# A hybrid encoder step: the beginning loaded in pairs of tiles, the odd mixer's normalisation split into shorter pieces, and the last output tile finished in two halves

## The chip, the cores and the metric

The kernel runs on one core of a Trainium2 chip. The metric is the device time of one execution in microseconds (us). The core has a matrix engine (PE, with its weight loads listed as PEld), a vector engine (DVE), a scalar engine (ACT), a general engine (POOL), and SP, which here issues DMAs; ACT issues some too.

## The reference, cut to what matters

Two layers over 384 tokens (256 of a prompt and 8 x 16 of samples), 1024 features, everything in fp32:

```python
x = x + 0.5 * swiglu(rmsnorm(x, g1), wg, wu, wd)      # ffn1, 1024 -> 2816 -> 1024
x = x + mixer(rmsnorm(x, g))                          # layer 0: even mixer, layer 1: odd mixer
x = x + 0.5 * swiglu(rmsnorm(x, g2), wg, wu, wd)      # ffn2
# odd mixer
u, vv, ga, gb = split(h @ w_in)
vv = layernorm(gelu(vv), ln_g, ln_b);  yc = gelu(u) * spatial_gate(vv, ws, bs)
cd = causal_dwconv(ga * sigmoid(gb), width 31)
yd = silu(layernorm(cd + dw_b, cn_g, cn_b))
y  = concat(yc, yd) @ w_out
# at the very end
y = rmsnorm(x, final_g)
```

## The kernel before, in words

Activations lie with features on the 128 partitions and the 384 tokens along the free dimension, so `x` is eight tiles `xT[k]` of 128x384. Every product is made three times: each fp32 operand is split into a rounded part and a rest (`xh`, `xl` for activations, `hi`, `lo` for weights), and `mm3` adds high x high, low x high and high x low in one PSUM bank. The split of a tile is a copy on ACT (the high part) and a subtraction on DVE (the rest).

**The stream.** All weights come as pieces of 128x1024, in order, through `Stream`: SP issues the load of a piece into one of four `raw` buffers, `fill_split` makes its `hi` (ACT, L247) and `lo` (DVE or POOL, L249) in one of three buffers each, and `get` hands out a piece, issues loads further ahead, and splits two pieces ahead of the one handed out. A new `hi` thus waits until PE is done with the piece three places earlier.

**The order of the work** is written out by hand. `proj_a` makes two 128x384 results (two pieces), `proj_b` four, `proj_tok` three of 128 tokens x 512 columns. Inside them `tick` and `tock` advance a clock, `clock['n']`; side work is hung on it with `at(n, fn)`, whole numbers in the middle of a piece, halves at its end. Each engine works through its instructions in program order. Results of PE go into four banks of the kind `pbank` and four of the kind `bank`; a `pbank` can be written again only when the evacuation of its last content is done.

**The beginning** (L314 to L542). ACT's queue loads `pcol` (all per-feature columns, 98 KB); SP's queue loads `x` and the first two weight pieces in turns, the first two feature tiles one by one, the others in pairs. Eight matmuls of ones run meanwhile (L517). A loop over the eight feature tiles `k` makes `xh` (ACT, L520), the piece's part `hi` (ACT, L267), `lo` (POOL, L268), `xl` (DVE, L522), and PE's six matmuls of `k` (L525, L532, L533), the last four one step behind.

**The RMS factor** is a chain: `rstd_split`, `rstd_sums` (a sum over partitions on PE, then a diagonal picked out and reduced on DVE, a power of -1/2 on POOL, four small DVE steps that refine it, a diagonal product, a split), `rstd_spread` (PE, ACT). `first` (L557) evacuates the first two pairs of results of the first ffn, where that factor was not yet there.

**The odd mixer** has PE ticks 0 to 3 for `vv` (`proj_tok`), 4 to 11 for `ga, gb` (`glu`), 12 to 15 for `u`, 16 to 19 for the first half of the output projection (`ych`, `ycl`: four pieces, called A to D below, A and B for the first four results, C and D for the other four), 20 to 23 for the second (`ydh`, `ydl`: E to H). Convolutions 1 to 3 run on PE at ticks 9, 11, 13 (`conv`), convolution 0 as `taps` on DVE. The layer norm of `cd` hangs on the clock:

```python
        at(LN[0], ln_1)                            # 14: mean, centred cd, squares
        at(LN[1], ln_2)                            # 15: sum of the squares, split
        at(LN[2], lambda: rstd_sums(onesc))        # 16.5
        at(LN[3], ln_3)                            # 18: factor, 4 x (product, silu, split)
```

The gates `gate(i)` (two at tick 16) give `ych[i]`, `ycl[i]`: a product on DVE, then ACT's copy, then DVE's rest.

**The end** (`last`). For each 512-column half `hf` and 128 tokens `t` PE sums 22 products; the last three pieces of the second half are held back so that the three `t` end one after the other. `evac` adds to `x` and squares, `norm` makes the factor and the two output halves, which SP stores.

Of the kernel before, what the change touches and what calls it, by code (L numbers as in the profile page):

```python
# [42 lines left out]
P = 128  # L43
NT = 384
# [8 lines left out]
LN = (14, 15, 16.5, 18)  # L53
# [6 lines left out]
TP = (2, 2, 2, 2, 8, 2, 2, 2, 7, 2)  # L60
# [54 lines left out]
def _layout(x):  # L115
# [9 lines left out]
    def feat(a, n):  # L125
# [9 lines left out]
        'x': feat(tok, KD),  # L135
        'cols': cols,
# [16 lines left out]
_INS = [('w', (len(_pieces()), P, 1024)), ('x', (P, KD, NT)), ('cols', (P, NCOL)), ('ck', (8, P, 4, NP)),  # L153
# [68 lines left out]
class Stream:  # L222
# [56 lines left out]
def encoder_step(ctx, tc, d_w, d_x, d_cols, d_ck, d_cv, d_clf, d_ssc, d_scc, d_wfl, d_ebf, d_lng, d_lnb, d_wst,  # L279
# [51 lines left out]
    A.activation(warm, warm, AF.Copy)  # L331
# [51 lines left out]
    def rsqrt(out, v, n, pw=P):  # L383

        G.tensor_tensor(out, v, nhalf[:pw, 0:n], op=ALU.pow)  # L385
        t = tmp(8)[:pw]
# [22 lines left out]
    def rstd_sums(scale=None):  # L409
# [11 lines left out]
        rsqrt(rc[:, 0:3], v[:, 0:3], 3)  # L421
        dg = tmp()
        V.tensor_tensor(dg.rearrange("p (t q) -> p t q", q=P), id3,
                        rc[:, 0:3].unsqueeze(2).to_broadcast([P, 3, P]), op=ALU.mult)
        rbox['d'] = split_tmp(dg)
        rbox['rc'] = rc
# [89 lines left out]
    for _ in range(8):  # L516
        mm(ps_first[0][:, 0:P], lhsT=ones1, rhs=ones1, start=True, stop=True)  # L517
    for k in range(KD + 1):
        if k < KD:
            A.activation(xh[k], xT[k], AF.Copy, scale=col('ffn1_g', k))  # L520
            st.part_split(k // 4, k % 4)
            V.scalar_tensor_tensor(xl[k], xT[k], col('ffn1_g', k), xh[k].bitcast(F32),  # L522
                                   op0=ALU.mult, op1=ALU.subtract)
            for n in range(2):
                mm(ps_first[n][:, 0:NT], lhsT=st.hl[k // 4][0][:, k % 4, n * P:(n + 1) * P], rhs=xh[k],  # L525
                   start=k == 0, stop=False)
        if k > 0:
            q = k - 1
            hi, lo = st.hl[q // 4]
            for n in range(2):  # L530
                c = slice(n * P, (n + 1) * P)
                mm(ps_first[n][:, 0:NT], lhsT=hi[:, q % 4, c], rhs=xl[q], start=False, stop=False)  # L532
                mm(ps_first[n][:, 0:NT], lhsT=lo[:, q % 4, c], rhs=xh[q], start=False, stop=q == 7)  # L533
        if k in (3, 7):
            tick()
# [4 lines left out]
    adma(out=cb, in_=c_big)  # L540
    for k in range(KD):
        square(k, V)  # L542
# [5 lines left out]
    def ffn(rp, gnext, lnext, extra=None, ps0=None, fresh=True):  # L548
# [469 lines left out]
    def odd(pre, first_piece, gnext, lnext):  # L1018
# [83 lines left out]

        def ln_sum():
# [31 lines left out]
        def conv_sum(i):  # L1135
# [270 lines left out]
```

## Time and profile before

| | |
|---|---|
| median of 3 runs | 1444.8 us (1443.97 to 1445.63) |
| the profiled execution | 1442.76 us |
| its span, first to last instruction | 1441.0 us |
| PE busy | 1420.0 us, 99% of the span |
| DVE, ACT, POOL busy | 759.3, 566.6, 140.2 us |
| mean granted clock of PE | 0.995 |
| read from HBM | 180.98 MB, 128 GB/s over the span |

A time of an instruction runs from its start to its modelled end; matmuls are pipelined, so they start closer together than they last. "Idle before" is time in which an engine had nothing to do, with what ended it. The granted clock is the share of the full 2.4 GHz that PE was allowed: 1.00 is 2.4 GHz, 0.50 is 1.2 GHz.

### The profile page before, as it was taken

What the parts mean: (1) busy time and instruction counts of PE and PEld (TensorE: products, weight loads), DVE (VectorE), ACT (ScalarE), POOL (GpSimd) and SP (SyncE); (2) the same over time, 40 slices, a digit from 0 to 9 for tenths busy, and PEclk for the clock granted to TensorE, in tenths of its full rate; (3) what the DMA queues carried; (4) which work ended last, traced back from release to release, by engine and by line L of the source; (5) the groups of instructions that cost most, each with busy time, mean ns of one, the idle gap of its engine ahead of it and who ended that gap; (6) DMA issues with size and microseconds to landing.
All of it is one profiled execution on the core that took longest, in us unless ns stands there. A gap on an engine that the chain in (4) does not pass through costs nothing. (4 is left out here: it accounts for less than half of the span.)

```text
span 1441.0 us, 21647 instructions
## 1 busy us (share of the span) xinstructions
PE 1420.0 (99%) x8916; PEld 1366.5 (95%) x8916; DVE 759.3 (53%) x1103; ACT 566.6 (39%) x842; POOL 140.2 (10%) x151
## 2 busy tenths in 40 slices
PE   9999999999999999999999999999999899999997
PEld 8999999998889999999999999999877899999886
DVE  6655544372346655553465555442686775555333
ACT  5433333255454433332334333332534443333332
POOL 3010000034335000000010100000000110000010
PEclk9999999999999999999999999999999999999999
DMA  6433333337433434333434443334322343333331
GB/s 219 136 120 134 127 123 130 127 111 263 162 116 113 140 117 132 132 117 132 131 117 133 152 136 131 128 114 147 110 90 67 103 147 132 117 131 132 114 125 69
DMA packets 54567, 186.53 MB, mean 129 GB/s; under 512 B 6692, under 2 KB 8700, under 8 KB 54468
## 3 DMA queue, kind: packets, MB, share of 16 engines
q1 hardware_dynamic: 51348, 175.35, 36.5%
q10 hardware_dynamic: 3024, 9.70, 2.0%
q8 instruction: 70, 1.15, 0.3%
q14 instruction: 29, 0.24, 0.1%
q0 software_dynamic: 96, 0.10, 0.0%
HBM read 180.98 MB, written 4.11 MB: 128 GB/s over the span
## 5 line engine op out<-in xcount | busy, mean ns | idle before, releaser
L249 DVE TENSOR_TENSOR lo<-raw,hi 128x1024 fp32r<-128x1024 f32 x294 | 366.1, 1251 | 422.1 <-ACT hi L247 422.0
L436 PE MATMUL b<-xh,hi 128*128 128x384 f32 x1648 | 555.5, 337 | 0.9 <-ACT vv L1193 0.5
L438 PE MATMUL b<-xh,lo 128*128 128x384 f32 x1648 | 553.1, 336 | 1.3 <-DVE lo L249 1.3
L437 PE MATMUL b<-xl,hi 128*128 128x384 f32 x1648 | 552.8, 335 | 0.0
L247 ACT ACTIVATE hi<-raw 128x1024 fp32r<-128x1024 f32 x318 | 333.5, 1054 | 369.0 <-PE b L437 180.7
L436 PEld LDWEIGHTS b<-xh,hi 128*128 128x128 f32 x1648 | 309.3, 188 | 7.1 <-issue 5.0
L438 PEld LDWEIGHTS b<-xh,lo 128*128 128x128 f32 x1648 | 309.2, 188 | 1.9 <-DVE lo L249 1.9
L437 PEld LDWEIGHTS b<-xl,hi 128*128 128x128 f32 x1648 | 309.3, 188 | 0.0
L436 PE MATMUL b<-gh,hi 128*128 128x384 f32 x528 | 176.9, 335 | 0.0
L438 PE MATMUL b<-gh,lo 128*128 128x384 f32 x528 | 176.9, 335 | 0.0
L437 PE MATMUL b<-gl,hi 128*128 128x384 f32 x528 | 176.9, 335 | 0.0
L368 ACT ACTIVATE gh<-t 128x384 fp32r<-128x384 f32 x88 | 46.2, 525 | 166.9 <-DVE t L593 165.6
L438 PEld LDWEIGHTS b<-gh,lo 128*128 128x128 f32 x528 | 99.2, 188 | 0.0
L436 PEld LDWEIGHTS b<-gh,hi 128*128 128x128 f32 x528 | 99.2, 188 | 0.0
L437 PEld LDWEIGHTS b<-gl,hi 128*128 128x128 f32 x528 | 99.2, 188 | 0.0
L577 ACT ACTIVATE t<-t 128x384 f32<-128x384 f32 x86 | 45.2, 526 | 132.6 <-DVE t L575 132.6
L375 POOL TENSOR_TENSOR acc<-acc,t 128x384 f32<-128x384 f32 x31 | 36.0, 1161 | 605.1 <-ACT t L373 603.5
L369 DVE TENSOR_TENSOR gl<-t,gh 128x384 fp32r<-128x384 f32 x88 | 49.2, 559 | 52.1 <-ACT gh L368 52.1
L575 DVE TENSOR_TENSOR t<-b,rstd 128x384 f32<-128x384 f32 x86 | 47.5, 553 | 54.7 <-PE b L438 54.7
L249 POOL TENSOR_TENSOR lo<-raw,hi 128x1024 fp32r<-128x1024 f32 x24 | 58.1, 2421 | 89.7 <-ACT hi L247 83.8
L436 PE MATMUL b<-hi,gh 128*128 128x512 f32 x132 | 51.4, 390 | 0.0
L437 PE MATMUL b<-lo,gh 128*128 128x512 f32 x132 | 51.4, 389 | 0.0
(294 smaller groups left out, 1144.3 us busy)
## 6 DMA issues: line engine op xcount, KB each, us to landing
raw<-in_w SPq DMA_DIRECT2D x318, 512.0 KB
kb<-in_ck ACTq DMA_DIRECT2D x8, 512.0 KB
vb<-in_cv ACTq DMA_DIRECT2D x8, 512.0 KB
out_y<-t SPq DMA_DIRECT2D x6, 256.0 KB
xT<-in_x SPq DMA_DIRECT2D x3, 384.0 KB
raw<-in_w SPq DMA_DIRECT2D x3, 256.0 KB
out_k<-kT SPq DMA_DIRECT2D x1, 768.0 KB
out_v<-vt ACTq DMA_DIRECT2D x3, 256.0 KB
```

What stands on the lines that cost most here:

```text
L247: nc.scalar.activation(hi, raw, AF.Copy)
L249: e.tensor_tensor(lo, raw, hi.bitcast(F32), op=ALU.subtract)
L368: A.activation(hi, src, AF.Copy)
L369: (eng or V).tensor_tensor(lo, src, hi.bitcast(F32), op=ALU.subtract)
L375: (E or G).tensor_tensor(acc, acc, sq, op=ALU.add)
L436: mm(ps, lhsT=wh, rhs=ah, start=first, stop=False)
L437: mm(ps, lhsT=wh, rhs=al, start=False, stop=False)
L438: mm(ps, lhsT=wl, rhs=ah, start=False, stop=last)
L575: V.tensor_tensor(t, psg[n][:, 0:NT], rbox['r'], op=ALU.mult)
L577: A.activation(s, t, AF.Silu)
```

## The change

It edits four places. *Beginning*: ffn1's first scale comes as its own small tensor `g0` on ACT's queue, `pcol` is loaded later, behind `cb`; the loads of `x` and of the weights go in pairs of tiles on SP's queue; the parts are split two at a time, the rest on DVE in place of POOL; nine matmuls of ones; the loop goes by pairs. *First ffn*: `first` makes both products for silu before it multiplies; the table of Silu is loaded at the start. *Odd mixer*: tables are loaded in another order (gelu at tick 0, sigmoid after the statistics of `vv`, silu at tick 16 in place of after `u`); 4 taps at tick 11 and 5 at tick 12 in place of 7 and 2 at 11 and 11.5; two adds (`ln_part`) move from `conv_sum(2)` to tick 13; `ln_2` comes after the evacuation of `u` in place of tick 15; at piece A nothing is split, and the split of C follows the gates at tick 16; the factor chain is cut at POOL's power (16.5 and 17.5); `yd` is made two tiles at a time (18.5, 19, 19.5). *End*: the last 128 tokens are finished in two column halves of 256, the second in a bank of its own; the refinement has two small steps in place of four (with -0.5 folded into the final scale `fg`); the first output half goes out on ACT's queue.

```diff
--- before.py
+++ after.py
-LN = (14, 15, 16.5, 18)
+LN = (14, 16.5, 17.5, 18.5, 19, 19.5)
-TP = (2, 2, 2, 2, 8, 2, 2, 2, 7, 2)
+TP = (2, 2, 2, 2, 8, 2, 2, 2, 4, 0, 5)
...
+        'g0': x['ffn1_g'][0].reshape(KD, P).T,
...
     def part_split(self, j, k):
         (hi, lo), raw = self.hl[j], self.raw[j]
+        k = slice(k, k + 2)
         self.nc.scalar.activation(hi[:, k], raw[:, k], AF.Copy)
-        self.nc.gpsimd.tensor_tensor(lo[:, k], raw[:, k], hi[:, k].bitcast(F32), op=ALU.subtract)
+        self.nc.vector.tensor_tensor(lo[:, k], raw[:, k], hi[:, k].bitcast(F32), op=ALU.subtract)
...
-    adma(out=pcol, in_=d_cols)
+    g0 = cp.tile([P, KD], F32, name="g0")
+    adma(out=g0, in_=d_g0)
     st.open(2)
-    for k in (0, 1):
-        dma(out=xT[k], in_=d_x[:, k])
-        st.part_dma(0, k, k + 1)
-    for k in (2, 4, 6):
+    for k in (0, 2, 4, 6):
         dma(out=xTt[k // 2], in_=d_x[:, k:k + 2])
         st.part_dma(k // 4, k % 4, k % 4 + 2)
...
-    A.activation(warm, warm, AF.Copy)
+    A.activation(warm, warm, AF.Silu)
...
-    def rstd_sums(scale=None):
+    def rstd_sums(scale=None, later=False):
...
-        rsqrt(rc[:, 0:3], v[:, 0:3], 3)
+        G.tensor_tensor(rc[:, 0:3], v[:, 0:3], nhalf[:, 0:3], op=ALU.pow)
+        rbox['n'] = rc, v
+        rbox['rc'] = rc
+        if not later:
+            rstd_diag()
+
+    def rstd_diag():
+        rc, v = rbox.pop('n')
+        newton(rc[:, 0:3], v[:, 0:3], 3)
         dg = tmp()
...
         rbox['d'] = split_tmp(dg)
-        rbox['rc'] = rc
...
-    def proj_b(ah, al, k0, nk, kfirst, klast, evac, after=lambda n: None):
+    def proj_b(ah, al, k0, nk, kfirst, klast, evac, after=lambda n: None, late=None):
...
-            wh, wl = st.get()
+            wh, wl = st.get(st.j + 2 if p0 == late else None)
...
-    for _ in range(8):
+    for _ in range(9):
         mm(ps_first[0][:, 0:P], lhsT=ones1, rhs=ones1, start=True, stop=True)
...
+    for k in range(0, KD, 2):
+        for q in (k, k + 1):
+            A.activation(xh[q], xT[q], AF.Copy, scale=g0[:, q:q + 1])
+            if q == k:
+                st.part_split(k // 4, k % 4)
+            V.scalar_tensor_tensor(xl[q], xT[q], g0[:, q:q + 1], xh[q].bitcast(F32),
                                    op0=ALU.mult, op1=ALU.subtract)
...
+        hh(k)
+        hh(k + 1)
+        hl_lh(k)
+        hl_lh(k + 1)
...
     adma(out=cb, in_=c_big)
+    adma(out=pcol, in_=d_cols)
...
+            s = [tmp(), tmp()]
             for n in range(2):
-                s = tmp()
-                V.tensor_tensor(s, pg[n][:, 0:NT], rbox['r'], op=ALU.mult)
-                A.activation(s, s, AF.Silu)
-                V.tensor_tensor(u[n], u[n], s, op=ALU.mult)
+                V.tensor_tensor(s[n], pg[n][:, 0:NT], rbox['r'], op=ALU.mult)
+                A.activation(s[n], s[n], AF.Silu)
+            for n in range(2):
+                V.tensor_tensor(u[n], u[n], s[n], op=ALU.mult)
                 split(u[n], gh[n], gl[n])
...
+        def ln_part():
+            t = lnb_['s'] = tmp()
+            V.tensor_tensor(t, cd[1], cd[2], op=ALU.add)
+            V.tensor_tensor(t, t, cd[0], op=ALU.add)
...
-            if i == 2:
-                t = lnb_['s'] = tmp()
-                V.tensor_tensor(t, cd[1], cd[2], op=ALU.add)
-                V.tensor_tensor(t, t, cd[0], op=ALU.add)
...
-        at(0, lambda: A.activation(warm, ones1[:, 0:2], AF.Sigmoid))
+        at(0, lambda: A.activation(warm, ones1[:, 0:2], AF.Gelu_apprx_tanh))
...
         vv_stats()
+        A.activation(warm, ones1[:, 0:2], AF.Sigmoid)
...
         def ln_3():
             rstd_spread()
-            rl = rbox['r']
-            for i in range(4):
-                V.tensor_tensor(cd[i], cd[i], rl, op=ALU.mult)
-            for i in range(4):
+            for i in range(2):
+                V.tensor_tensor(cd[i], cd[i], rbox['r'], op=ALU.mult)
+
+        def ln_4():
+            for i in range(2):
+                t = lnb_[i] = tmp()
+                A.activation(t, cd[i], AF.Silu, scale=col('o_cn_g', i), bias=col('o_cn_b', i))
+                A.activation(ydh[i], t, AF.Copy)
+            ln_lo(0)
+
+        def ln_lo(i):
+            V.tensor_tensor(ydl[i], lnb_.pop(i), ydh[i].bitcast(F32), op=ALU.subtract)
+
+        def ln_5():
+            for i in range(2, 4):
+                V.tensor_tensor(cd[i], cd[i], rbox['r'], op=ALU.mult)
+            for i in range(2, 4):
                 t = tmp()
                 A.activation(t, cd[i], AF.Silu, scale=col('o_cn_g', i), bias=col('o_cn_b', i))
                 split(t, ydh[i], ydl[i])
...
-        at(LN[1], ln_2)
-        at(LN[2], lambda: rstd_sums(onesc))
+        at(13, ln_part)
+        at(16, lambda: st.fill_split(st.j + 2))
+        at(16, lambda: A.activation(warm, ones1[:, 0:2], AF.Silu))
+        at(LN[1], lambda: rstd_sums(onesc, True))
+        at(LN[2], rstd_diag)
         at(LN[3], ln_3)
+        at(LN[4], ln_4)
+        at(LN[5], ln_5)
...
-        A.activation(warm, ones1[:, 0:2], AF.Silu)
+        ln_2()
...
-            proj_b(ych, ycl, 0, 4, 0, 3, evac)
+            proj_b(ych, ycl, 0, 4, 0, 3, evac, lambda n: hf == 1 and n == 0 and ln_lo(1), late=-hf)
...
+            V.tensor_scalar(fg, fg, -0.5, None, op0=ALU.mult)
...
             def norm(t):
...
-                rsqrt(rs[:, t:t + 1], v, 1)
+                v, r, u = ss[:, 5 * t + 2:5 * t + 3], rs[:, t:t + 1], ss[:, 5 * t + 4:5 * t + 5]
+                G.tensor_tensor(r, v, nhalf[:, 0:1], op=ALU.pow)
+                V.scalar_tensor_tensor(u, r, v, r, op0=ALU.mult, op1=ALU.mult)
+                V.scalar_tensor_tensor(r, u, -3.0, r, op0=ALU.add, op1=ALU.mult)
...
-                dma(out=outs[t][:, 0:512], in_=o)
+                adma(out=outs[t][:, 0:512], in_=o)
...
+                    if hf and t == 2:
+
+                        for j in range(3):
+                            step(ps[t], t, ws[j], kt + 2 * j, slice(0, 256))
+                        end = pbank()
+                        for j in range(3):
+                            step(end, t, ws[j], kt + 2 * j, slice(256, 512), kt)
+                        evac(ps[t], t, 512, 256)
+                        down_add(ps[t], t, 768, 256)
+                        evac(end, t, 768, 256)
```

Here `hh(k)` issues the two high x high matmuls of tile `k` and `hl_lh(k)` the four others; `newton` is the four small steps that stood in `rsqrt`; `step`, `down_add` and `evac` of the end take the columns they work on, and `evac` squares on ACT and adds up the sums on DVE.

## Rows read from the trace of the kernel before

**Rows 1.** Page, parts 1 and 5 (busy us, mean ns of one | idle before).

```profile
PE 1420.0 (99%) x8916; PEld 1366.5 (95%) x8916; DVE 759.3 (53%) x1103; ACT 566.6 (39%) x842; POOL 140.2 (10%) x151
...
L249 DVE TENSOR_TENSOR lo<-raw,hi 128x1024 fp32r<-128x1024 f32 x294 | 366.1, 1251 | 422.1 <-ACT hi L247 422.0
...
L247 ACT ACTIVATE hi<-raw 128x1024 fp32r<-128x1024 f32 x318 | 333.5, 1054 | 369.0 <-PE b L437 180.7
```

**Rows 2.** Waits of PE: who waited for whom, us in total, times, longest.

```profile
PE b L436 <- DVE xT L1288: 4.5, 2, 2.3
PE b L436 <- ACT ych L368: 2.2, 2, 1.8
PE a L525 <- ACT hi L267: 1.8, 2, 1.6
PE b L438 <- DVE lo L249: 1.3, 2, 0.6
...
PE a L357 <- ACT xt L1312: 0.7, 1, 0.7
PE a L1124 <- ACT GP L1168: 0.6, 1, 0.6
PE b L436 <- ACT vv L1193: 0.5, 1, 0.5
```

**Rows 3.** Windows by stage: length, busy us (instructions), granted clock, DMA.

```profile
0.00:17.63 17.63, 14.72 (x64) 13.69 (x65) 10.46 (x18) 13.23 (x28) 7.51 (x12) 0.90 0.84 290
17.63:72.00 54.37, 53.34 (x300) 52.70 (x300) 34.88 (x54) 22.58 (x33) 4.92 (x12) 1.00 0.42 141
...
1028.00:1108.55 80.55, 78.58 (x1089) 65.51 (x1088) 57.41 (x93) 35.92 (x66) 0.85 (x1) 1.00 0.28 90
1108.55:1147.00 38.45, 31.57 (x171) 28.99 (x171) 23.95 (x43) 15.93 (x24) 3.33 (x9) 0.91 0.24 82
...
1433.50:1441.00 7.50, 0.02 (x1) 0.00 (x0) 2.23 (x7) 1.44 (x3) 0.54 (x1) 0.67 0.36 140
...
1160.00:1334.00 174.00, 174.00 (x1006) 174.00 (x1005) 98.56 (x136) 65.62 (x88) 1.97 (x2) 1.00 0.38 127
```

**Rows 4.** Timeline of the beginning: start us, us, engine, line, operation.

```profile
1.09 3.78 PE L517 MATMUL a<-ones 128*128 128x128 f32 x16 [1.09 <-DVE ones L347]
...
3.80 0.61 ACT L520 ACTIVATE xh<-xT,pcol 128x384 fp32r<-128x384 f32 x1 [1.12 <-DMA pcol<-in_cols]
...
6.87 0.42 ACT L267 ACTIVATE hi<-raw 128x256 fp32r<-128x256 f32 x1 [1.23 <-DMA raw<-in_w]
...
9.52 0.52 PE L532 MATMUL a<-xl,hi 128*128 128x384 f32 x1
...
33.35 1.28 ACT L565 ACT_TABLE_LOAD   x1 [1.60 <-DVE t L564]
```

**Rows 5.** Timeline of DVE and PE in the odd mixer's output projection.

```profile
1108.02 1.73 DVE L1244 TENSOR_TENSOR t<-t,t 128x384 f32<-128x384 f32 x3
...
1116.08 0.55 DVE L1227 TENSOR_TENSOR t<-a,ut 128x384 f32<-128x384 f32 x1
...
1118.83 0.56 DVE L369 TENSOR_TENSOR ycl<-t,ych 128x384 fp32r<-128x384 f32 x1 [0.59 <-ACT ych L368]
...
1121.60 0.18 DVE L388 TENSOR_TENSOR t<-rcol 128x3 f32<-128x3 f32 x1 [0.76 <-POOL rcol L385]
...
1125.87 1.94 DVE L1288 TENSOR_TENSOR xT<-b,xT 128x384 f32<-128x384 f32 x4
...
1137.89 0.41 PE L436 MATMUL b<-ydh,hi 128*128 128x384 f32 x1 [2.35 <-DVE xT L1288]
```

**Rows 6.** Timeline of the end, and of the transposes ahead of it.

```profile
1342.59 1.14 PE L357 MATMUL a<-cb,xT 128*128 128x128 f32 x8 [0.69 <-ACT xt L1312]
...
1433.56 0.69 DVE L1324 SCALAR_TENSOR_TENSOR xt<-b,xt 128x512 f32<-128x512 f32 x1 [0.44 <-PE b L438]
...
1437.69 0.38 SPq L1341 DMA_DIRECT2D out_y<-t  x1
```

More of the change, by code (lines that the diff above doesn't have):

```diff
@@ L385, in rsqrt, with newton @@
         G.tensor_tensor(out, v, nhalf[:pw, 0:n], op=ALU.pow)
+        newton(out, v, n, pw)
+    def newton(out, v, n, pw=P):
         t = tmp(8)[:pw]
@@ L515, in encoder_step, with hh, hl_lh @@
     ps_first = [bank(), bank()]
-    for _ in range(8):
+    for _ in range(9):
         mm(ps_first[0][:, 0:P], lhsT=ones1, rhs=ones1, start=True, stop=True)
[L518 to L522, printed above, removed]
-                                   op0=ALU.mult, op1=ALU.subtract)
[L524 to L534, printed above, removed]
+    def hh(k):
+        for n in range(2):
+            mm(ps_first[n][:, 0:NT], lhsT=st.hl[k // 4][0][:, k % 4, n * P:(n + 1) * P], rhs=xh[k],
+               start=k == 0, stop=False)
+    def hl_lh(k):
+        hi, lo = st.hl[k // 4]
+        for n in range(2):
+            c = slice(n * P, (n + 1) * P)
+            mm(ps_first[n][:, 0:NT], lhsT=hi[:, k % 4, c], rhs=xl[k], start=False, stop=False)
+            mm(ps_first[n][:, 0:NT], lhsT=lo[:, k % 4, c], rhs=xh[k], start=False, stop=k == 7)
+    for k in range(0, KD, 2):
[4 more added lines that the diff above has]
+            V.scalar_tensor_tensor(xl[q], xT[q], g0[:, q:q + 1], xh[q].bitcast(F32),
+                                   op0=ALU.mult, op1=ALU.subtract)
+        hh(k)
+        hh(k + 1)
+        hl_lh(k)
+        hl_lh(k + 1)
+        if k in (2, 6):
             tick()
@@ L1322, in evac @@
[L1322 to L1327 removed]
+                    mm3(ps[:, c], gh[k][:, t * P:(t + 1) * P], gl[k][:, t * P:(t + 1) * P],
+                        w[0][:, kk, c], w[1][:, kk, c], k == k0, k == KF - 1)
@@ new lines, in down_add, with evac @@
+            def down_add(ps, t, c0, n):
+                xx = xt[t][:, c0:c0 + n]
+                V.scalar_tensor_tensor(xx, ps[:, c0 % 512:c0 % 512 + n], 0.5, xx, op0=ALU.mult, op1=ALU.add)
+            def evac(ps, t, c0, n):
+                xx = xt[t][:, c0:c0 + n]
+                down_add(ps, t, c0, n)
+                sq = tmp(512)
+                q = ss[:, 5 * t + 3:5 * t + 4]
+                A.activation(sq[:, 0:n], xx, AF.Square, accum_out=q)
+                j = 0 if c0 == 0 else 1 if c0 + n < D else 2
+                v = ss[:, 5 * t + j:5 * t + j + 1]
+                if j == 0:
@@ L1328, in evac @@
                     G.tensor_tensor(xx, xx, fg[:, 0:512], op=ALU.mult)
-                    V.tensor_scalar(ss[:, 2 * t:2 * t + 1], ss[:, 2 * t:2 * t + 1], 1.0 / D, EPS, op0=ALU.mult, op1=ALU.add)
+                    V.tensor_scalar(v, q, 1.0 / D, EPS, op0=ALU.mult, op1=ALU.add)
+                else:
+                    p = ss[:, 5 * t + (j - 1 if c0 > 512 else 0):5 * t + (j - 1 if c0 > 512 else 0) + 1]
+                    V.scalar_tensor_tensor(v, q, 1.0 / D, p, op0=ALU.mult, op1=ALU.add)
@@ L1348, in down @@
                     for t in range(3):
-                        step(ps, t, w, p0)
+                        step(ps[t], t, w, p0)
                     tick()
@@ L1352, in down @@
                 for t in range(3):
-                    for j in range(ntail):
-                        step(ps, t, ws[j], KF - 2 * ntail + 2 * j)
-                    evac(ps, t, hf)
+                    kt = KF - 2 * ntail
+                    if hf and t == 2:
[7 more added lines that the diff above has]
+                        evac(end, t, 768, 256)
+                    else:
+                        for j in range(ntail):
+                            step(ps[t], t, ws[j], kt + 2 * j)
+                        evac(ps[t], t, 512 * hf, 512)
                     if hf:
```

25 lines of the change are left out of this document (8 added, 17 removed).

## The prediction

> **What bounds the kernel now.** I read the page first: PE is busy 1420.0 of 1441.0 us [rows 1], so all that an edit of order can give lies in 21 us of idle time, and in stretches where PE is busy at half its clock. The waits of PE say where the idle time is: 11.6 us stand in seven named waits, the largest on DVE's evacuation of `xT` and on ACT's `ych` in the odd mixer [rows 2], 7.5 behind the last matmul and 1.1 ahead of the first [rows 3, 4]. The windows by stage then price each place [rows 3]. The beginning, up to the end of the first 48 matmuls, takes 17.63 us with PE busy 14.72, so 2.9 idle, at a mean clock of 0.90, worth 17.63 x 0.10 = 1.8 more. The first ffn's start loses 54.37 - 53.34 = 1.0. The odd mixer up to its output projection loses 80.55 - 78.58 = 2.0. The output projection and a little of the next ffn loses 38.45 - 31.57 = 6.9 idle and 38.45 x 0.09 = 3.5 to the clock. The last 7.5 us have no matmul but the end of one. From 1160 to 1334 PE never stops, one matmul per 174.00 / 1006 = 0.173 us: nothing is to be had there. The sum is made against the profiled execution, 1442.8 us (1441.0 of span and 1.8 around it); the median of the timed runs is 2.0 above it, and I carry this distance over.
>
> **Beginning.** The real matmuls waited 1.8 us for the copies `hi` [rows 2], which waited for loads: `xh` of tile 0 started at 3.80, when `pcol` had landed, and the second `hi` only at 6.87, when its weights had [rows 4]. After that gap the matmuls ran for a while at the half clock, 1.2 GHz (one lasts 0.52 at 9.52). In the new order the first two tiles and their weights are the same 640 KB, in two issues in place of four and without the 98 KB of `pcol` beside them; they land between 3.80 (the first arrival seen) and 6.87. I take 5.0, nearer to the early end because fewer issues stand in front. The eight matmuls of ones took 3.78, so nine end at 1.09 + 9 x 0.47 = 5.3; the pair's copy takes about 0.6, between the 0.42 of 128x256 and 1.05 of 128x1024 [rows 1, 4], so PE starts at 5.6. Then 48 x 0.173 = 8.3, and 0.4 for the first `xl`, which now stands behind the pair's rest on DVE: the stage ends at 14.3 in place of 17.63, **-3.3**. With PE kept busy from 1.1 on I expect no half clock. DVE takes four pair rests over from POOL, about 0.7 each by the 0.69 of a 128x512 [rows 6], 2.8 in all, against 2.1 us of PE work per pair, so they hide. Bounds: -3.6 (both losses gone) and -0.5 (weights at 6.87, and the clock falls again). `pcol` goes past `cb` on ACT's queue; its first reader is hundreds of matmuls later, in the side work of tick 16.
>
> **First ffn.** The table load of 1.28 at 33.35 [rows 4] and two of the four hand-overs between DVE and ACT (0.6 each, as in [rows 5]) leave `first`: 2.5 us. The waits behind it, 1.0 in all, are for `hi` and `lo` queued behind `first` on ACT and DVE. PE comes 3.3 earlier, but the factor chain that starts `first` follows PE too. **-1.0**; bounds -1.0 and 0.
>
> **Odd mixer, up to the output projection.** Gelu's table is there when `vv` is evacuated, so 1.28 goes and with it the wait of 0.5 on `vv`; sigmoid's table is loaded behind the statistics, ahead of two splits, where ACT has room, so `glu` is 1.28 earlier and the 0.6 on `lo` (one of the two waits of L438) goes. Convolution 3 waited 0.6 for `GP`, which on DVE stood behind 7 + 2 taps and two adds; now 4 taps are ahead of it [rows 2]. Together **-1.9** with the rounding of the windows; bounds -2.0 and -0.5. What is late next would be the 5 taps moved behind, but they have until tick 13.
>
> **The output projection.** I follow DVE, in the old times, from PE's first matmul on `ych` at 1108.55. Before: `ln_2` (three adds, 1.73), its split, `u`, the rest of a piece (1.25), then the gates: product at 1116.08, the last `ycl` done at 1118.83 + 0.56 = 1119.4; the two gates take 3.3 [rows 5]. PE had asked for `ych[2]` 1.8 us before it came at about 1117.2, so at 1115.4. Now: `u` 1.0 from about 1108.2 (1109.4 with PE's last result), `ln_2` 1.73 and its split 1.1 to 1112.2, gates 3.3 to 1115.5: just in time, no wait. Then `lo` of C with its hand-over 1.6 (1117.1), the first part of the factor chain 0.55 + 0.55 + 0.2 (1118.4), `lo` of D 1.25 (1119.7); the wait of 0.76 for POOL and the rest of the chain now come behind the evacuations, the first of which ends at 1120.2. PE ends B at 1115.4 + 24 x 0.173 = 1119.6, so 0.6 of idle time is left where 2.1 was. The four evacuations take 1.94 (1121.6), the chain's second part about 2.5 (four small steps of 0.2, a product of 0.55, a split of 1.1; 1124.1); PE reaches its sum at 1120.2 + 4.2 = 1124.4. `lo` of E and two products, 2.2, then `lo` of F 1.25, one evacuation, two rests and three evacuations interleaved to about 1130.9; `ydl[0]` at 1129, `ydl[1]` at 1130. PE begins E at 1129.0 with about 0.2 of waits, in place of 1137.89 behind 2.35 [rows 5], and G and H follow with 0.3. That is 8.7 earlier, and 1.7 more for the half clock after 1137.89 (half of 3.5): 10.4. By the windows, 10.3 of loss less 1.1 left over is 9.2. I take the middle, **-9.7**; bounds -10.4 and -4.
>
> **The end.** PE's last 18 matmuls of 512 columns become 36 of 256. No row has this form; the nearest are 128-wide transposes, 8 in 1.14, 0.14 each [rows 6], and 0.173 for 384. So 36 cost 5.1 at 0.14 where 18 cost 4.1 (0.173 x 512 / 384 each): +1.0 on PE. It is partly covered: DVE must still finish `norm(1)`, then add a half (about 0.42, from the 0.69 of 512), wait for ACT's square, add two more halves and wait again. I get the power at 0.5 later than before, two small steps fewer (-0.2), and the second store no longer 0.4 behind the first on SP (its issue stood at 1437.69), but the bytes of both then leave together. **+0.3**; bounds -0.4 and +2.1 (36 x 0.173 = 6.2). `fg` times -0.5 costs up to 1.25 (a 128x1024 on DVE), while PE waits on ACT's `xt` [rows 2]; uncovered it would cost that.
> The Trainium skill, *TensorE: Matmul & The Clock Gate*, section on the back-to-back issue gap, gives N / 2.4 GHz + 2.5 ns, 109 ns for 256 columns, and 107 ns for a 128-column weight load; by it 36 cost 3.9, and the sum at the end would be 0 or a little less. At 384 columns it gives 162 where the trace has 173, so I stay with the rows.
>
> **Sum**: -3.3 - 1.0 - 1.9 - 9.7 + 0.3 = -15.6. The profiled execution would be 1427.2; with the 2.0 of the timed runs, 1429.2: **1429**.
>
> **The rivals.** (a) *The beginning gives nothing*: the pair of weights lands as late as 6.87, PE pauses after the ones, the clock falls as before. For it: DMA was at 0.84 of its time in that stage [rows 3]. Against: fewer bytes are in front. -15.6 + 3.3 - 0.3, so 1432.2. (b) *DVE takes the place of what was removed*: my schedule leaves only 0.6 us between DVE and PE at C and E. If the evacuations are still 2 us late at both, 4.4 of idle and one half clock (1.7) remain, 10.3 - 6.1 = 4.2 of gain, total 1434.7. For it: DVE was busy 23.95 of 38.45 there. Against: the chain's 0.76 wait and its second part surely leave the path. (c) *The tables come back*: ACT's sigmoid load ahead of the splits holds them up, so that the 0.6 on `lo` stays: 1429.8. The Trainium skill, *ScalarE: Activation LUTs*, section on what a table load costs, says that a switch is the 1.28 load and a drain of 1.38, 2.66 in all, which would do this; the trace shows 1.28 at 33.35, with the load's idle time ahead of it put down to DVE, so little speaks for it. (d) *Nothing moves*: each removed wait reappears at the next link (a PE that is 99% busy says so of most of the span): 1444.8. (e) *Slower*: the split of C held back at A is never caught up, so that from B to H PE waits in each of seven pieces for a copy and a rest, 1.05 + 1.25 + 0.4 = 2.7, 18.9 in place of 10.3, and with PE busy 4.2 of 6.9 us the clock is half for a tenth of those 48 us, 2.4: 1444.8 - 5.9 + 8.6 + 2.4 = 1449.9. It decides when `lo` of C comes after PE has ended B (1119.6); I have it at 1117.1.
>
> **How the numbers follow.** Forecast 0.62, (a) 0.13, (b) 0.15, (c) 0.03, (d) 0.04, (e) 0.03. Terms at their best give -17.4, so 1427.4, and if the timed runs lie at their profile, 2.0 less; so the low end is 1425.4. To leave out no more than two in ten the high end takes in (a) and most of (b): 1435. A difference of 0.2%, 2.9 us, is about what timing can tell from no change. Faster: forecast, (a), (b), (c), 0.93; same: (d) 0.04; slower: (e) 0.03.
>
> **What would show it.** Right: PE's first matmul on real data before 6, the first stage over near 14.3 with the clock at 1.00; no wait on `vv` or `GP`; the waits on `xT` and `ych`, 6.7 before, together under 1.5, and no half clock in the output projection; from the last matmul to the end about as long as before. Wrong: waits of PE on DVE of 2 us at C or E; a granted clock of 0.5 anywhere before the last store; 36 narrow matmuls in over 5.5 us.

## The result, and the profile after

The changed kernel takes 1430.3 us, the median of four runs (1428.21 to 1433.03), beside 1444.4 for the kernel before: a ratio of 0.9906, with a 95% interval of 0.9886 to 0.9927. In a second set of five runs it took 1428.6 (1428.29 to 1429.41), 0.9899 with 0.9883 to 0.9916. It is faster by about 1%, 14 us; the forecast was 1429.0. The profiled execution took 1428.2 with a span of 1426.4, so the spans differ by 1441.0 - 1426.4 = 14.6, where the sum was 15.6.

Four marks that both kernels have divide that difference: the first matmul of the stage behind the beginning, the first on `ych`, the first of the ffn behind the output projection, and the start of the last matmul.

| stretch | before | after | difference | term of the prediction |
|---|---|---|---|---|
| start to the end of the first stage | 17.63 | 14.95 | -2.68 | -3.3 |
| to the first matmul on `ych` | 1090.92 | 1088.11 | -2.81 | -1.0 - 1.9 |
| to the first matmul behind the output projection | 47.63 | 37.59 | -10.04 | -9.7 |
| to the start of the last matmul | 276.95 | 277.33 | +0.38 | +0.3, with the next row |
| from there to the end | 7.87 | 8.42 | +0.55 | |

The waits of PE in the changed kernel, all that the view lists (who waited for whom: us in total, times, longest):

```profile
PE a L527 <- DVE ones L347: 1.1, 1, 1.1
PE a L357 <- ACT xt L1352: 0.7, 1, 0.7
PE a L530 <- ACT hi L269: 0.7, 1, 0.7
PE b L446 <- DVE xT L1327: 0.5, 1, 0.5
PE b L448 <- DVE lo L250: 0.2, 1, 0.2
```

Beside [rows 2], the waits on `ych`, `GP` and `vv` are gone, that on `xT` went from 4.5 to 0.5 and that on `lo` from 1.3 to 0.2. The wait on `xt`, in front of which the new product of `fg` was put, is still 0.7. The windows by stage (length; busy time of PE, PEld, DVE, ACT, POOL; granted clock; DMA share; GB/s), to be read against [rows 3]:

```profile
0.00:14.95 14.95, 13.07 (x66) 12.25 (x67) 9.62 (x21) 11.50 (x21) 0.20 (x4) 1.00 0.88 320
14.95:69.30 54.35, 54.31 (x313) 53.99 (x313) 36.45 (x56) 23.68 (x35) 4.93 (x12) 1.00 0.45 148
1023.50:1103.06 79.56, 79.27 (x1091) 66.33 (x1091) 58.07 (x93) 34.64 (x66) 0.85 (x1) 1.00 0.29 91
1103.06:1140.65 37.59, 37.12 (x223) 35.64 (x223) 31.80 (x53) 21.70 (x34) 7.95 (x12) 1.00 0.40 121
1160.00:1320.00 160.00, 160.00 (x925) 160.00 (x924) 88.28 (x117) 60.08 (x79) 0.00 (x0) 1.00 0.39 127
```

[rows 3] ends its window of the output projection nine us short of the next ffn. The whole stretch before:

```profile
1108.55:1156.18 47.63, 40.75 (x224) 38.17 (x223) 32.72 (x54) 22.45 (x36) 6.88 (x13) 0.93 0.31 101
```

PE is idle for 0.5 us in the output projection where it was for 6.9, and the granted clock is 1.00 where 0.93 stood; in the beginning it is 1.00 where 0.90 stood (ahead of 5.48 us that 1.00 is no record, see the last section). Beginning and output projection gave back idle time and clock together. A clock of 0.50 is on record from 1422.01 on, ahead of the last store, which by its letter is a sign that the prediction called wrong; it stands four us behind the last matmul and costs nothing. The timeline of the beginning (start, duration, engine, line, operation):

```profile
1.08 4.21 PE L527 MATMUL a<-ones 128*128 128x128 f32 x18 [1.08 <-DVE ones L347]
4.52 0.61 ACT L542 ACTIVATE xh<-xT,g 128x384 fp32r<-128x384 f32 x1 [1.84 <-DMA g<-in_g]
5.27 0.63 ACT L269 ACTIVATE hi<-raw 128x512 fp32r<-128x512 f32 x1
5.95 1.13 PE L530 MATMUL a<-xh,hi 128*128 128x384 f32 x4 [0.66 <-ACT hi L269]
```

`xh` waited for the 4 KB of `g` until 4.52, later than it had for the 98 KB of `pcol` [rows 4]; whether that set the start is tried below. In the output projection the evacuation at C comes at 1113.92, ahead of the chain's second part, and PE waits 0.46 for it:

```profile
1112.78 1.23 DVE L250 TENSOR_TENSOR lo<-raw,hi 128x1024 fp32r<-128x1024 f32 x1
1112.87 1.84 POOL L424 TENSOR_TENSOR rcol<-t,nhalf 128x3 f32<-128x3 f32 x1 [75.80 <-DVE t L422]
1113.92 1.94 DVE L1327 TENSOR_TENSOR xT<-b,xT 128x384 f32<-128x384 f32 x4
1114.61 0.41 PE L446 MATMUL b<-ych,hi 128*128 128x384 f32 x1 [0.46 <-DVE xT L1327]
```

The end, from the sum of the first half of the last tile. The last matmul starts at 1417.98:

```profile
1417.42 0.42 DVE L1365 SCALAR_TENSOR_TENSOR xt<-b,xt 128x256 f32<-128x256 f32 x1
...
1417.84 0.35 ACTq L1391 DMA_DIRECT2D out_y<-t  x1
...
1418.24 0.42 ACT L1373 ACTIVATE t<-xt 128x256 f32<-128x256 f32 x1 [0.43 <-DVE xt L1365]
...
1418.78 0.16 DVE L1381 SCALAR_TENSOR_TENSOR ss<-ss 128x1 f32<-128x1 f32 x1 [0.94 <-ACT t L1373]
1418.86 0.95 DVE L1365 SCALAR_TENSOR_TENSOR xt<-b,xt 128x256 f32<-128x256 f32 x2
1419.90 0.42 ACT L1373 ACTIVATE t<-xt 128x256 f32<-128x256 f32 x1 [1.15 <-DVE xt L1365]
...
1420.68 0.54 POOL L1386 TENSOR_TENSOR rsf<-ss,nhalf 128x1 f32<-128x1 f32 x1 [4.41 <-DVE ss L1381]
```

DVE stands idle for 0.94 us ahead of its small step on the first half, which needs ACT's square; the sums of the second half are queued behind that step. The square starts 0.40 behind the end of its sum. Here a store that ACT issues lies between; in the kernel with `g` in `x`'s rows (below) that store was issued 0.28 sooner, counted from the last matmul, and the square started no sooner, so the store isn't shown to hold it up.

### The profile page after: what moved, and what is told of

The parts are those of the page before. It is cut to its first block, busy times and chain, and to the rows that moved or that the text cites. A ratio compares the mean times of both kernels' runs of the same rounds, so it can differ in the third digit from the quotient of the medians.

```text
span 1426.4 us, 21672 instructions
## 1 busy us (share of the span) xinstructions
PE 1414.9 (99%) x8936; PEld 1364.1 (96%) x8936; DVE 758.8 (53%) x1105; ACT 563.9 (40%) x839; POOL 135.1 (9%) x143
## 3 DMA queue, kind: packets, MB, share of 16 engines
q8 instruction: 70, 1.15, 0.3%
## 4 chain that ended last, share of the span: by engine, by line
PE 96%; ACT 1%; DVE 1%; issue 1%; DMA 0%; POOL 0%; POOLq 0%; SPq 0%; ACTq 0%
PE b L446 30%; PE b L448 30%; PE b L447 30%; PE a L1148 1%; PE a L357 1%; PE a L884 1%; ACT hi L248 0%; PE a L796 0%; DVE lo L250 0%; PE a L814 0%; DMA raw<-in_w 0%; PE a L1244 0%; PE a L537 0%; PE a L538 0%; PE a L401 0%
## 5 line engine op out<-in xcount | busy, mean ns | idle before, releaser
L446 PE MATMUL b<-hi,gh 128*128 128x512 f32 (+1 forms) x138 | 52.5, 380 | 0.0
L447 PE MATMUL b<-lo,gh 128*128 128x512 f32 (+1 forms) x138 | 52.4, 380 | 0.0
```

Source lines behind the costliest of these rows:

```text
L446: mm(ps, lhsT=wh, rhs=ah, start=first, stop=False)
L447: mm(ps, lhsT=wh, rhs=al, start=False, stop=False)
```

## The experiments

Each is the changed kernel with one thing undone or added. All have the same marks, and the stretches are compared by them; where nothing was edited, the output projection differs from the first profile by up to 0.3 us, the stretch from the first stage to `ych` by up to 0.9 and the last ffn by up to 3.5, so each part is judged by its own stretch and not by the whole span. From the start of the last matmul to the end, profiles with the same end lie between 8.0 and 8.5. Three expectations name a stretch of 28.90 us, of which no view shows the ends; they are judged by the stretch from the first matmul on `ych` to the first on `ydh` (20.38 in the changed kernel) and by the whole output projection (37.59).

### Parts undone one by one

**The beginning as before.** Tiles 0 and 1 singly with their weights, factors from `pcol`, rests on POOL, eight matmuls of ones.

```
-    for k in (0, 2, 4, 6):
+    for k in (0, 1):
+        dma(out=xT[k], in_=d_x[:, k])
+        st.part_dma(0, k, k + 1)
+    for k in (2, 4, 6):
...
-        self.nc.vector.tensor_tensor(lo[:, k], raw[:, k], hi[:, k].bitcast(F32), op=ALU.subtract)
+        self.nc.gpsimd.tensor_tensor(lo[:, k], raw[:, k], hi[:, k].bitcast(F32), op=ALU.subtract)
```

> The changed kernel with the beginning as it was before (tiles 0 and 1 singly, factors from pcol, rests on POOL, eight matmuls of ones), all else as changed. My theory, that the beginning is a term of its own: the first matmul of the next stage comes at about 17.6 us in place of 14.95, the half clock of some 3 us near 9 to 12.6 is back, and the span is 2.7 us longer than 1426.4, so about 1429.1. Rival, that the later start is caught up by work that waits for something else behind it: the stage ends at 17.6, but the span is less than 1.5 longer.

The first stage ended at 17.07, the span was 1428.8, +2.4. Windows of it, the first stage and three us within it:

```profile
0.00:17.07 17.07, 14.50 (x64) 13.62 (x65) 10.41 (x18) 13.07 (x28) 7.63 (x12) 0.90 0.87 307
9.00:12.00 3.00, 3.00 (x11) 3.00 (x11) 2.87 (x4) 3.00 (x8) 2.92 (x4) 0.50 1.04 405
```

The granted clock is 0.50, the 1.2 GHz level, behind a wait of 0.90 us for `hi`. The beginning is a term of its own, 2.1 here and 2.7 against the profile of before. That the span comes out 2.4 longer is luck: up to `ych` 0.7 of the 2.1 is gone again, and the last ffn, where nothing was edited, is 1.5 longer. Both are the pace of the matmuls (last section). PE's idle time from the first stage to `ych` is 0.3 in either kernel, so no wait behind the beginning took up the later start. The beginning was undone as a whole; which of its edits carries it is not shown.

**The split of C at A's get again.**

```
-        at(16, lambda: st.fill_split(st.j + 2))
...
-            proj_b(ych, ycl, 0, 4, 0, 3, evac, lambda n: hf == 1 and n == 0 and ln_lo(1), late=-hf)
+            proj_b(ych, ycl, 0, 4, 0, 3, evac, lambda n: hf == 1 and n == 0 and ln_lo(1))
```

> The changed kernel, but the copy and rest of piece C are issued at A's get again, ahead of the gates. My theory: DVE has 1.25 us and ACT 1.05 more ahead of the last two gates, PE waits 1.0 to 2.0 us for ych within B, and if so a half clock of up to 1.7 can follow; the stretch of the output projection (28.90 us, idle 0.5) grows by 1.0 to 3.5. Rival, that taking u's evacuation first was enough: no wait on ych, stretch within 0.3 of 28.90.

From the first matmul on `ych` to the first on `ydh` it took 20.98 us, +0.60; the whole output projection 37.94, +0.35. Between the two theories: short waits on `ych` came back, and the wait at C shrank in their place.

```profile
1110.73 0.44 PE L446 MATMUL b<-ych,hi 128*128 128x384 f32 x1 [0.40 <-ACT ych L368]
...
1114.92 0.19 PEld L446 LDWEIGHTS b<-ych,hi 128*128 128x128 f32 x1 [0.18 <-DVE xT L1326]
```

**`ln_2` at tick 15 again**, ahead of `u`'s evacuation.

```
+        at(15, ln_2)
...
-        ln_2()
```

> The changed kernel, but ln_2 (three adds of 1.74 us in all and a split) is at tick 15 again, ahead of the evacuation of u. My theory: u's products and so the gates come up to 2.3 us later, PE waits 1 to 2.3 us at A or B for b's banks or ych, stretch 1 to 4 us longer with the clock's loss. Rival, that DVE has 2 us free ahead of u's last result: stretch within 0.3 of 28.90.

The stretch was 20.33, -0.05, and the output projection 37.25: no effect, my theory falls. (The span, 1430.3, was 3.9 longer; 3.45 of that is in the last ffn, where nothing was edited. The last section comes back to it.)

**Both of these undone together.**

```
-        at(16, lambda: st.fill_split(st.j + 2))
+        at(15, ln_2)
...
-        ln_2()
...
-            proj_b(ych, ycl, 0, 4, 0, 3, evac, lambda n: hf == 1 and n == 0 and ln_lo(1), late=-hf)
+            proj_b(ych, ycl, 0, 4, 0, 3, evac, lambda n: hf == 1 and n == 0 and ln_lo(1))
```

> The changed kernel with two of the parts undone together: ln_2 at tick 15 again and the split of C at A's get again (each alone changed the stretch from the first matmul on ych to the first on ydh, 20.38 us, by -0.05 and +0.60). Theory, that the two stand in for each other, and that either one alone leaves DVE just enough time for the gates: undone together the wait on ych of the kernel before is back, 1.8 to 2, and with the clock up to 2.7, so 22.2 to 23.1. Rival, that neither matters and only the cut chain did: the sum of the two, 20.4 to 21.0.

```profile
1112.65 0.44 PE L446 MATMUL b<-ych,hi 128*128 128x384 f32 x1 [0.35 <-ACT ych L368]
...
1113.25 0.44 PE L447 MATMUL b<-ycl,hi 128*128 128x384 f32 x1 [0.15 <-DVE ycl L369]
...
1114.27 0.44 PE L446 MATMUL b<-ych,hi 128*128 128x384 f32 x1 [0.41 <-ACT ych L368]
```

21.89, +1.51, and 38.81 for the output projection, +1.22: more than the two alone (0.55), less than the full wait. So the two parts stand in for each other to a good part. Either one gives DVE and ACT most of the time that the gates need.

**The factor chain in one piece**, at tick 16.5, ahead of the evacuations.

```
-        at(LN[1], lambda: rstd_sums(onesc, True))
-        at(LN[2], rstd_diag)
+        at(LN[1], lambda: rstd_sums(onesc))
```

> The changed kernel, but the factor chain is one piece again, at tick 16.5, so that DVE stands behind POOL's power and does the small steps, the product and its split ahead of the four evacuations. My theory: the first evacuation, at 1113.92 now, comes 2.5 to 4 us later (power 0.85 to 1.84, four steps 0.6, product 0.66, split 1.1), PE waits that much more at C than 0.46 now, and a half clock of up to 1.7 follows: stretch 28.90 + 2.5 to 5.5. Rival, that the chain was covered anyway: under 0.7 longer.

```profile
1113.48 0.85 POOL L424 TENSOR_TENSOR rcol<-t,nhalf 128x3 f32<-128x3 f32 x1 [75.75 <-DVE t L422]
1114.36 0.19 DVE L391 TENSOR_TENSOR t<-rcol 128x3 f32<-128x3 f32 x1 [0.76 <-POOL rcol L424]
...
1118.63 1.94 DVE L1326 TENSOR_TENSOR xT<-b,xT 128x384 f32<-128x384 f32 x4
1119.32 0.66 PE L446 MATMUL b<-ych,hi 128*128 128x384 f32 x1 [4.56 <-DVE xT L1326]
```

The stretch took 26.66, +6.28, above my range, and the output projection 43.59 at a clock of 0.92, +6.0. PE waits 4.56 at C, longer than it did before the change (2.14 at that place); that is 4.1 of the 6.0, and most of the rest is the half clock that follows, 0.50 from 1117.2 to 1124.0. Counted from its first matmul on `ych`, PE comes to C at 11.1, where it came at 15.8 before the change, and DVE's evacuation starts at 15.0, where it started at 17.3. PE gained 4.7 and DVE 2.3, so much of the old lateness shows again in one wait.

**`yd` four at a time**, at tick 18.5.

```
-            for i in range(2):
+            for i in range(4):
                 V.tensor_tensor(cd[i], cd[i], rbox['r'], op=ALU.mult)
...
-        at(LN[4], ln_4)
-        at(LN[5], ln_5)
```

> The changed kernel, but yd is made four at a time at tick 18.5 (four products of 0.55 in one block, then four activations each with its copy and rest). My theory, by which yd two at a time is part of the gain: the two more products hold up the rest of E and the first ydh or ydl by 1.1 us, PE waits 0.7 to 1.5 at D or E, ych to the first matmul of the next ffn 37.59 + 0.7 to 2.5 with the clock. Rival, that the cut chain alone made the room: within 0.3 of 37.59.

```profile
1120.46 1.97 DVE L1271 TENSOR_TENSOR cd<-cd,rstd 128x384 f32<-128x384 f32 x4
...
1127.91 1.95 DVE L1311 TENSOR_TENSOR xT<-b,xT 128x384 f32<-128x384 f32 x4
1128.61 0.66 PE L446 MATMUL b<-ydh,hi 128*128 128x384 f32 x1 [4.48 <-DVE xT L1311]
```

The output projection took 43.10 at a clock of 0.96, +5.5, twice what I allowed; 4.5 of it is the wait at E. I had counted the two products more. What counts is that all four products and rests, each rest behind a hand-over from ACT, stand ahead of the evacuation: from 1120.46 to 1127.91, and no bank comes free meanwhile.

**The table loads where they were**, all but Silu's at tick 16.

```
-    A.activation(warm, warm, AF.Silu)
+    A.activation(warm, warm, AF.Copy)
...
-        at(0, lambda: A.activation(warm, ones1[:, 0:2], AF.Gelu_apprx_tanh))
+        at(0, lambda: A.activation(warm, ones1[:, 0:2], AF.Sigmoid))
...
-        A.activation(warm, ones1[:, 0:2], AF.Sigmoid)
```

> The changed kernel with the table loads where they were (Copy in place of Silu at the start, Sigmoid in place of Gelu at tick 0, none behind the statistics). My theory: 1.28 us of load come back into each of the two chains, PE's waits of up to 1.0 in the first ffn and of 0.55 on vv and 0.6 on lo in the odd mixer return; from the first stage's end to the first matmul on ych 1088.11 + 1.0 to 2.2. Rival, that ACT has room for the loads in the new order: within 0.4 of 1088.11.

From the first stage's end to `ych` it took 1090.60, +2.49. The waits of PE in that stretch, where the changed kernel has one of 0.2:

```profile
PE b L448 <- DVE lo L250: 1.0, 3, 0.6
PE b L446 <- ACT vv L1213: 0.5, 1, 0.5
PE a L401 <- DVE t L369: 0.2, 1, 0.2
```

Idle time of PE rose by 1.4 there, in line with my theory. That is about half of what the whole change took away in this stretch (3.0 before, 0.3 now): the 0.5 on `vv` and the 0.6 on `lo` in the odd mixer are back, and 0.3 of the 1.0 that the first ffn had lost. The other 1.1 is a slightly slower pace of the matmuls, which I do not put down to the loads: PE is busy for 1088.9 in this stretch and for 1088.7 in the kernel with both small parts undone, which has the new loads (1087.8 in the changed kernel).

### The end

**Without the halves**: 18 matmuls of 512 columns for the last tile, the rest of the new end kept.

```
-                    if hf and t == 2:
+                    if False:
```

> The changed kernel, but the last output tile is made by 18 matmuls of 512 columns and evacuated whole, with the rest of the new end (two small steps, store on ACT's queue, fg by -0.5). From the start of the last matmul to the end the kernel before took 7.87 us, the changed one 8.42. Theory, that the halves themselves lengthen the end, because DVE's small step on the first half's sum waits for ACT's square with the second half's sums queued behind it: 7.87 less two small steps (0.2 each) and less the second issue on SP (0.3), so 7.2 to 7.5. Rival, that the halves do shorten it and something else in the new end costs: 8.5 or more.

From the start of the last matmul to the end 7.93 in place of 8.42, and the stretch ahead of it 277.03 in place of 277.33: the halves cost 0.8 us against the first profile of the changed kernel. Two other profiles with halves ended in 8.0 and 8.2, the square on the first half starting 0.27 sooner (why is open), so 0.4 to 0.8. My 7.2 to 7.5 was too low. Two small steps fewer are worth 0.12 (from the start of POOL's power to the product 1.03, before 1.15), and the second store on ACT's queue gives nothing: product to end is 4.76, before 4.57. The bytes of the two stores leave together anyway, and in both kernels they are done 1.5 to 1.7 before the span's end.

**All sums and squares of the halves ahead of DVE's small steps**, together with three edits at the beginning (`g` in `x`'s rows, `xl` ahead of the pair's rest on DVE, ten matmuls of ones).

```
-    for _ in range(9):
+    for _ in range(10):
...
-            if q == k:
-                st.part_split(k // 4, k % 4)
             V.scalar_tensor_tensor(xl[q], xT[q], g0[:, q:q + 1], xh[q].bitcast(F32),
                                    op0=ALU.mult, op1=ALU.subtract)
+            if q == k:
+                st.part_split(k // 4, k % 4)
...
-                        evac(ps[t], t, 512, 256)
+                        evac(ps[t], t, 512, 256, 1)
                         down_add(ps[t], t, 768, 256)
-                        evac(end, t, 768, 256)
+                        evac(end, t, 768, 256, 1)
+                        evac(ps[t], t, 512, 256, 2)
+                        evac(end, t, 768, 256, 2)
```

> The changed kernel with four edits: g in x's rows, xl ahead of the pair's rest on DVE (PE waited 0.5 for it), ten matmuls of ones, and at the end all sums and squares of the halves ahead of DVE's small steps on them. Theory: first stage over at 14.0 to 14.6 in place of 14.95; from the start of the last matmul to the end 7.6 to 7.8 in place of 8.42, since DVE no longer waits for a square with two sums behind it; profiled span about 1425, timed median 1.0 to 2.0 below the changed kernel's. Rival, that both gains are taken back by other waits: median within 0.7 of the changed kernel's.

```profile
1421.36 1.31 DVE L1369 SCALAR_TENSOR_TENSOR xt<-b,xt 128x256 f32<-128x256 f32 x3
...
1422.18 0.42 ACT L1378 ACTIVATE t<-xt 128x256 f32<-128x256 f32 x1 [0.71 <-DVE xt L1369]
...
1422.70 0.42 ACT L1378 ACTIVATE t<-xt 128x256 f32<-128x256 f32 x1
...
1423.48 0.54 POOL L1393 TENSOR_TENSOR rsf<-ss,nhalf 128x1 f32<-128x1 f32 x1 [3.27 <-DVE ss L1388]
```

The new last argument parts `evac`: 1 is the sum and the square, 2 the small step on it. The last matmul starts at 1421.92; three sums run without a gap and the power comes 1.56 behind it in place of 2.70. To the end it takes 7.28, -1.14, more than I gave it. Against the wide form that is 7.28 + 0.30 - 7.93 = -0.35. Each of the two forms has one profile, and equal ends differ by up to 0.45, so that halves pay in this order is likely and not shown. This order does beat the other one, which ended in 8.0 to 8.5. The beginning gained nothing, its stage ended at 15.40 (the reason is in the next part). The timed median was 1429.6 (1427.37 to 1431.75), beside 1428.6 for the changed kernel on the same chip, so a kernel that beats it is not shown; the lowest times, 1427.37 and 1427.88, lie 0.9 and 0.4 below its lowest.

### What sets the first matmul

**`g` behind `x`'s first pair, in the same rows of one load.**

```
+    x0 = cp.tile([P, 2 * NT + KD], F32, name="xT0")
+    g0 = x0[:, 2 * NT:]
...
-    adma(out=g0, in_=d_g0)
```

> The changed kernel, but the factors g of the first stage lie behind x's first pair of tiles in the same rows of one load (3104 bytes a row), in place of a load of their own of 32 bytes a row. In the eight profiles with the new beginning xh waited for g by name until 4.14 to 4.52 us, and the first real matmul came at 5.63 to 6.18. Theory A, that g's small rows hold up the beginning: xh at 3.6 to 3.9, first real matmul at 5.1 to 5.4. Theory B, that the first pair of weights is what comes last: the first hi still begins at 4.9 to 5.5 and the first real matmul at 5.6 to 6.2.

```profile
3.97 0.61 ACT L545 ACTIVATE xh<-xT 128x384 fp32r<-128x384 f32 x1 [1.74 <-DMA xT<-in_x]
5.06 0.63 ACT L269 ACTIVATE hi<-raw 128x512 fp32r<-128x512 f32 x1 [0.48 <-DMA raw<-in_w]
5.74 1.12 PE L533 MATMUL a<-xh,hi 128*128 128x384 f32 x4 [0.74 <-ACT hi L269]
```

`xh` came 0.2 to 0.5 earlier, `hi` did not: it waits for the weights. The stage ended at 14.96. Theory B holds; in the eleven other profiles with the new loads, `hi` began at 4.95 to 5.50.

**Eleven matmuls of ones.**

```
-    for _ in range(9):
+    for _ in range(11):
```

> The changed kernel with eleven matmuls of ones in place of nine, so that PE ends them at 1.09 + 11 x 0.47 = 6.2 us and goes into the real matmuls without a pause. In two of eight profiles the first 12 real matmuls took 0.32 us each in place of 0.173, behind a pause of 0.6 to 0.9. Theory, that the pause decides it: no slow matmul here, first stage over at 14.9 to 15.2, and timed runs at most 1 us above the better ones of the changed kernel. Rival, that the rate falls without a pause too: stage over at 16 or later in this profile.

No slow matmul in this profile, stage over at 15.12, timed median 1429.1 (five runs at 1428.41 to 1429.23, one at 1432.14). The profile fits my theory; the run at 1432.14 doesn't, as the theory allowed 1 us (the pace in the last section can do as much). Nor is it proof: nine of the other profiles with the new loads had a pause and no slow matmuls either. What sets them apart from the two slow ones is in the last section.

**The changed kernel once more.**

> The changed kernel once more. Its timed runs were 1428.2, 1428.6, 1432.0 and 1433.0. In the profiles so far, stretches of 40 us in the first ffn hold 231 matmuls with the new beginning and 233 with the old one, and in the last ffn 228 to 233. Theory, that the pace belongs to the execution: the times fall into two groups some 4 us apart again and this profile shows other counts in the last ffn than 233. Rival, that it belongs to the program: 231 and 233 again, and times within 1 us of each other.

Stage over at 15.22, the marks after it within 0.3 of the first profile (1088.39, 37.31, 277.46, 8.42), 925 matmuls again between 1160 and 1320. The times, 1428.29 to 1429.41, speak for the rival; that an execution can bring another pace is seen in other kernels (below), so neither is settled.

## Why the prediction was right

**Beginning, -3.3 (measured -2.7).** The direction held, and the granted clock does not fall in this profile. That it is the fewer issues ahead of the first weights which bring them sooner was not tried alone. The step that was off is the landing time. I took 5.0; `hi` began at 5.27 and the first real matmul came at 5.95 in place of 5.6. The pair's copy (0.63, taken as 0.6) and the wait for the first `xl` (0.45, taken as 0.4) were right; another 0.3 went in shorter waits. "With PE kept busy from 1.1 on I expect no half clock" leaves the start out: by their pace the ones start at 1.2 GHz in every profile, PE pauses behind them, and in two of the later profiles the real matmuls ran at 1.2 GHz too, up to 10 us (last section). The profiled execution was not one of these, which cost 1.4 us more.

**First ffn and odd mixer up to `ych`, -2.9 (measured -2.81).** Of the 2.8, 2.7 is idle time of PE that went. The tables carry about half of it, as the experiment with the old places shows: 1.4 comes back with them. The Trainium skill, *ScalarE: Activation LUTs*, section on what a table load costs, would have had a switch take 2.66; the traces here show 1.28 for a load, and PE's wait on `vv` and its longest on `lo`, back with the old places, are 0.5 and 0.6, as in [rows 2]. That the taps freed `GP` (0.6) was not tried alone; its wait is absent from every profile with the new taps. Nor was the new order in `first`, to which the rest would fall: of the 1.0 in the first ffn only 0.3 came back with the tables.

**Output projection, -9.7 (measured -10.04).** The schedule that followed DVE was right in its order and within a microsecond of its times: a wait of 0.46 at C where 0.6 was expected, none at E, G and H where 0.2 and 0.3 were, no half clock. The second part of the chain and POOL's power (1.84 long now, 0.85 where DVE waits for it) lie behind the evacuations and cost nothing. What I had not seen is how the parts hang together: the cut chain and `yd` in pairs are each worth 5.5 to 6.0 when the other is there, more than half of the whole 10.0, and the deferred split and `u` first are worth little singly and 1.2 together. The gain cannot be shared out among the parts. Rival (b), a new bound on DVE, is what each of the two big parts leaves when it is missing, with a wait of PE of 4.5 at one place, where [rows 2] has two of up to 2.3.

**End, +0.3 (measured +0.9, of which 0.55 behind the last matmul's start).** Two sizes were off in opposite ways. A narrow matmul takes 0.120 (36 from 1413.79 to 1417.98), not the 0.14 that I took from the transposes, so PE's part is +0.3 and not +1.0. The Trainium skill, *TensorE: Matmul & The Clock Gate*, section on the back-to-back issue gap, gives 109 ns, for matmuls without weight loads between them, and was nearer than my row. By its sum I would have forecast 0 at the end, and been further off: the path ran through DVE. The half's small step waits for a square, and two sums wait behind it, 1.1 us by the reordered kernel. I had the power 0.5 later, the longer PE part included; by the trace it comes 0.9 later, 0.4 ahead of the last matmul's start and 0.55 behind it, and I did not see that the order alone made the 0.55.

The sum was 1.0 too large: 0.6 from the beginning, 0.6 from the end, less 0.3 from the output projection. No rival's mechanism has a part in it. The 2.0 between the profile and the median, carried over from the kernel before, was 2.1 in the first set of runs and 0.0 in the second, so there the forecast of the median had luck.

## What to carry to other kernels

When an engine that feeds TensorE is late at several places in a row, removing one lateness can move the wait to the next place, here 4.5 us at one place where two waits of 2.1 and 2.4 had been; cut the chains at all of them, and don't add up what single parts are worth: undone one by one in the finished kernel, two of them gave back 5.5 and 6.0 of 10.0. Put what frees a bank (the evacuation) ahead of any step that waits for another engine, and where work is split in halves, queue the first half's dependent steps behind the second half's independent ones (1.1 us here). A load's own wait in the trace does not say that it sets the start: move it, and see whether the next operation, here the one that waits for the weights, comes earlier.

## What the runs showed of the hardware

The pace of back-to-back matmuls at a granted clock of 1.00 isn't fixed. Between 1160 and 1320 us, in the last ffn, the changed kernel does 925 matmuls of 384 columns; the kernel with the reordered end and the one with the early `ln_2` did 907 and 908, and the one with the old beginning 918, with nothing edited in that stretch. The reordered kernel:

```profile
1160.00:1320.00 160.00, 160.00 (x907) 160.00 (x906) 87.51 (x116) 58.54 (x77) 0.00 (x0) 1.00 0.36 126
```

That is 0.1764 us a matmul in place of 0.1730, 2%; from the first matmul behind the output projection to the start of the last it makes 3.4 us (280.78 in place of 277.33). The timed runs of the reordered kernel fall into two groups about 3.5 us apart (1427.4 to 1428.2 and 1431.0 to 1431.8), and the first four of the changed kernel do as well; that the pace is the cause there too is likely, and not shown. Between 80 and 280 us the pace goes with the program: 1154 and 1155 matmuls with the old beginning (0.1733 us each), 1147 to 1149 with the new one (0.1742 us). What sets it stays open.

A granted clock of 1.00 in the first microseconds can be no record at all. The trace's records of the clock begin where it first rises to 1.00, and the windows count the time ahead of that as 1.00. In twelve of the fourteen profiles the first record begins between 4.12 and 6.01 us; in the kernel with both small parts undone and in the one with the wide end it begins at 10.40 and 10.11. The pace of the matmuls says what the clock was ahead of it. In the kernel with the early `ln_2` the record begins at 4.12; the instructions of the ones start every 0.213 us ahead of it and every 0.111 behind it:

```profile
2.12:4.12 2.00, 2.00 (x11) 2.00 (x11) 0.00 (x0) 0.55 (x2) 0.00 (x0) 1.00 0.94 297
4.12:4.72 0.60, 0.60 (x6) 0.48 (x5) 0.00 (x0) 0.53 (x1) 0.00 (x0) 1.00 0.99 360
```

In the kernel with both small parts undone the first real matmuls start every 0.32 us up to 10.40, which is the pace of the kernel with the old beginning between 9 and 12 us, where 0.50 is on record, and every 0.173 behind it:

```profile
6.40:10.40 4.00, 4.00 (x14) 3.88 (x13) 3.23 (x7) 3.24 (x6) 0.00 (x0) 1.00 1.03 395
10.40:14.40 4.00, 4.00 (x25) 4.00 (x24) 4.00 (x7) 3.79 (x8) 0.00 (x0) 1.00 0.95 343
```

So by its pace PE starts at 1.2 GHz in every profile, and in these two it kept that level into the real matmuls; their first stage ended at 16.4, in the others with the new beginning at 14.7 to 15.4. The length of PE's pause behind the ones does not tell them apart (0.61 and 0.88 us in the slow two, 0.35 to 0.86 in nine others). What does is whether the clock had risen by the pause: in the nine it rose before the ones ended or within 0.2 us behind them, in the slow two it had not. With eleven ones it rose at 6.01, later than nine ones end (5.3) and just before the eleven did (6.14). That more ones keep the slow start away is likely from this, and not shown by one profile.
